# Seven products in place of eight for three of eight K pairs of the first MLP product and, in two passes over the columns, for six of 32 K pairs of the second

## The chip, the cores and the metric

One Trainium2 chip, one of its cores. The metric is the device time of one execution in microseconds (us); lower is better. The core has TensorE (PE, with its weight loads as PEld), VectorE (DVE), ScalarE (ACT), GpSimd (POOL) and SyncE (SP), which here only issues DMAs.

## The reference, cut to what matters

A layer of a streaming encoder on 256 tokens with D = 2048: an RMSNorm, a token mixer (two groups of eight heads each), an output projection, and then the squared-ReLU MLP, which is all that the change touches:

```python
h = h + hybrid_token_mixer(rms_norm(h, norm_mix_w), ...)      # 256 x 2048
n = rms_norm(h, norm_ffn_w)
h = h + jnp.square(jax.nn.relu(n @ w_ff1)) @ w_ff2            # 2048 -> 8192 -> 2048
return rms_norm(h, norm_final_w)
```

Everything is float32. The two MLP products have 256 x 2048 x 8192 multiplications each.

## The kernel before, in words

**A float32 product as three.** TensorE multiplies in the rounded format fp32r. The kernel splits each float32 operand into `hi`, a copy that ACT rounds (line 120), and `lo = w - hi`, which DVE computes (line 121), and adds hi·hi + lo·hi + hi·lo. One *product* below (`product`, lines 774 to 778) is these three matmuls of 128 x 128 weights against 512 columns into one PSUM bank. `split_pair` (its `split` has lines 120 and 121) splits 1024 columns of weights into a pair of buffers; five such pairs are used in turn, three from `spool` and two from `wp2`. So a split may run ahead of TensorE by as much as five pairs hold.

**Order.** A scheduler of the framework orders each engine's instructions when the kernel is built; on the chip each engine runs its own list in that order, and semaphores hold an instruction until its operands and buffers are there. Weights come as 1 MB tiles (`w`, three buffers), one DMA each from SP's queue.

**First MLP product** (lines 805 to 868). Eight column groups `ng` of 1024 columns; in each, eight K pairs `kp` of 256 rows, one weight tile each. A *plain pair* (`plain_quad`) takes eight products: two K halves by two token halves (128 rows) by two column halves (512). A *sum pair* (`kp` in `SUMS = (2, 5)`, lines 834 to 862) treats the same work as a 2 x 2 by 2 x 2 block product and takes seven products of sums of blocks, in the manner of Strassen and Winograd. For its weights DVE computes differences of its blocks, 2048 columns in all (`TT`, lines 840, 843 and 844), and 3584 columns have to be split instead of 2048: three pairs and one half pair `hi4`, `lo4`. The sums of activation blocks are made once (`blocks`, lines 713 to 734; the DVE lines 729 to 732): those of kp 0 to 3 during the output projection, those of kp 4 to 7 in the first group, where `fill` slips them between the products. Four of the seven products go to four PSUM banks `M` of their own, three go directly into the four banks `E` of the plain pairs; after the last sum pair, ACT copies one bank and DVE joins the four (lines 858 to 862), and at the group's end DVE adds each `E` bank (line 865). ReLU and a transpose with a square (`turn`, lines 783 to 790) leave the activations for the second product in `g`. `E` and `M` change their PSUM halves (`acc`, `accb`) from group to group.

**Second MLP product** (lines 870 to 945). 64 K tiles `f` of 128 rows, one weight tile of 2048 columns each, all eight banks as sums: 24 matmuls per tile (`ff2`, line 896), no sum pairs. The activations of a tile are split to `gs` (256 columns, lines 120 and 121). The last three tiles are held back (`held`, `TAIL = 3`), so that the sums are finished bank by bank: for token half 0 four banks, for token half 1 three banks and the last one in two pieces of 256 columns, nine matmuls each.

**The end.** For each finished bank `piece` (lines 947 to 952) adds to `h`, squares and weights; `row_rstd` takes the row's scale (with a power on POOL, line 963), `scaled` multiplies and issues the output DMAs (lines 967 to 972).

Of the kernel before, what the change touches and what calls it, by code (L numbers as in the profile page):

```python
# [7 lines left out]
F32 = mybir.dt.float32  # L8
F32R = mybir.dt.float32r
# [6 lines left out]
P = 128  # L16
# [59 lines left out]
def hybrid_block(ctx: ExitStack, tc: tile.TileContext, x, xt, w_in, w_ab, params, w_out, w_ff1, w_ff2,  # L76
# [594 lines left out]
    wp2 = ctx.enter_context(tc.tile_pool(name="wp2", bufs=2, side="right"))  # L671
    t1 = ExitStack()
# [12 lines left out]
    SUMS = (2, 5)  # L685
    sets = bpool.tile([P, 8192], F32R, tag="xT", name="sets")
    sets2 = tp.tile([P, 1792], F32R, tag="s2", name="sets2")
# [83 lines left out]
    def g(f, n=1):  # L771
        return gt[f // NG][:, f % NG:f % NG + n, :]
# [10 lines left out]
    def turn(ng, n, src, acc):  # L783

        half, hf = n // 2, n % 2
        pt = acc()
        for c in range(4):
            PE.transpose(pt[:, c * P:(c + 1) * P], src[:, c * P:(c + 1) * P], ident)  # L788
        ACT.activation(g(8 * ng + 4 * half, 4)[:, :, hf * P:(hf + 1) * P], pt.rearrange("p (c t) -> p c t", c=4),
                       AF.Square)  # L790

    def plain_quad(E, st, B, first, last, n_fill):

        def one(n, kk):
            hf, c = divmod(n, 2)
            a = [st[:, kk, s + hf * P:s + hf * P + P] for s in (0, T)]
            product(E[n], a, B[kk][c], first and kk == 0, last and kk == 1)

        for n, kk in [(n, kk) for n in range(4) for kk in range(2)] if last else \
                [(n, kk) for kk in range(2) for n in range(4)]:  # L800
            one(n, kk)
            if (n, kk) == (3, 0):
                fill(n_fill)

    c1 = ExitStack()
    for ng in range(NGR):
# [5 lines left out]
        for kp in range(KP):  # L812
            w = wtile()
            SP.dma_start(w, w_ff1[ng * KP + kp])
            if kp not in SUMS:
                B12, B11 = halves(split_pair(w[:, 0:1024]))
                B21, B22 = halves(split_pair(w[:, 1024:2048]))
                plain_quad(E, a_plain(kp), ((B11, B12), (B21, B22)), kp == 0, kp == KP - 1, 0 if kp == 0 else 2)
                if kp == 0:
                    fill(2)  # L820
                if ng == 0 and kp == 1:
# [8 lines left out]
                    gt += [fp.tile([P, NG, T], F32, tag=f"g{i}", name=f"g{i}") for i in range(2)]  # L830
# [5 lines left out]
            TT = tp.tile([P, 2048], F32, tag="TT", name="TT")  # L836
            B = [w[:, c * 512:(c + 1) * 512] for c in range(4)]
            T1, T2, T4 = [TT[:, c * 512:(c + 1) * 512] for c in (0, 2, 3)]
            B21, B22 = halves(split_pair(w[:, 1024:2048]))
            DVE.tensor_tensor(out=TT[:, 0:1024].rearrange("p (a c) -> p a c", a=2), in0=view(w, 0, [[1536, 2], [1, 512]]),  # L840
                              in1=view(w, 512, [[-512, 2], [1, 512]]), op=ALU.subtract)
            B1, B3 = halves(split_pair(TT[:, 0:1024]))
            DVE.tensor_tensor(out=T2, in0=B[3], in1=T1, op=ALU.subtract)
            DVE.tensor_tensor(out=T4, in0=B[2], in1=T2, op=ALU.subtract)
            B2, B4 = halves(split_pair(TT[:, 1024:2048]))
            B11 = [tp.tile([P, 512], F32R, tag=t, name=t) for t in ("hi4", "lo4")]
            split(B[1], None, *B11)
            st = a_sums(kp)
            A = [(st[:, 0, n, :], st[:, 1, n, :]) for n in range(7)]
            p1, p5, p6, p7 = M  # L850
            a0, z0 = kp == SUMS[0], kp == SUMS[-1]
            for dst, a, b in ((E[0], 1, B21), (E[1], 6, B22), (p5, 3, B1), (p7, 5, B3), (p6, 4, B2), (E[2], 2, B4),
                              (p1, 0, B11)):
                m = a in (0, 3, 4, 5)
                product(dst, A[a], b, a0 and m, z0 and m)
            if z0:
                C4 = cp.tile([P, 4, 512], F32, tag="C", name="C4")
                ACT.copy(C4[:, 0], p1)
                DVE.tensor_tensor(out=C4[:, 1], in0=p6, in1=C4[:, 0], op=ALU.add)
                DVE.tensor_tensor(out=C4[:, 2], in0=p5, in1=C4[:, 1], op=ALU.add)  # L860
                DVE.tensor_tensor(out=C4[:, 3], in0=p7, in1=C4[:, 2], op=ALU.add)
                DVE.tensor_tensor(out=C4[:, 1], in0=p7, in1=C4[:, 1], op=ALU.add)
# [13 lines left out]
    accs = [[None] * 4, [None] * 4]  # L876

    def columns(q, bank):
        for hf in range(2):
            for c in (2 * q, 2 * q + 1):  # L880
                accs[hf][c] = bank()

    columns(0, bank_m)
    TAIL = 3
    held = []

    def ff2(f, hf, c, gs, hl, fresh=None):

        hi, lo = hl[c // 2]
        at, n = (c % 2) * 512, 512  # L890
        dst, first, last = accs[hf][c], f == 0, f == (NF - TAIL - 1 if (hf, c) == (1, 3) else NF - 1)
        if fresh:
            dst, at = fresh[0], at + fresh[1]
            n, first, last = 256, f == NF - TAIL, f == NF - 1
        for a, ww in ((0, hi), (T, hi), (0, lo)):
            PE.matmul(dst, lhsT=gs[:, a + hf * P:a + hf * P + P], rhs=ww[:, at:at + n],  # L896
                      start=(first and a == 0 and ww is hi), stop=(last and ww is lo))

    keep = None
    late = []  # L900
    for f in range(NF):
        w = wtile()
        SP.dma_start(w, w_ff2[f])
        gs = f2.tile([P, 2 * T], F32R, tag="gs", name="gs", bufs=4)
        split(g(f)[:, 0, :], None, gs[:, 0:T], gs[:, T:])
        n = f - (NF - TAIL)
        if n == 0:
            keep = fp.tile([P, TAIL - 1, 2, D], F32R, tag="g0", name="keep")
        if f < 2:

            hl = [split_pair(w[:, 0:1024]), None]
            for hf in range(2):
                for c in range(2):
                    ff2(f, hf, c, gs, hl)
                    fill(f == 0 and hf == 1)
            fill(2)
            late.append((f, gs, w))
            if f == 1:
                columns(1, bank_e)
                c1.close()  # L920
                for f_, gs_, w_ in late:
                    hl = [None, split_pair(w_[:, 1024:2048])]
                    for hf in range(2):
                        for c in (2, 3):
                            ff2(f_, hf, c, gs_, hl)
            continue
        hl = []
        for q in range(2):
            qs = slice(q * 1024, (q + 1) * 1024)
            if 0 <= n < TAIL - 1:  # L930
                hl.append(split(w[:, qs], None, keep[:, n, 0, qs], keep[:, n, 1, qs]))
            else:
                hl.append(split_pair(w[:, qs]))
        if n >= 0:
            held.append((f, gs, hl))
            continue
        for q in range(2):
            for hf in range(2):
                for c in (2 * q, 2 * q + 1):
                    ff2(f, hf, c, gs, hl)  # L940
# [111 lines left out]
```

## Time and profile before

| | |
|---|---|
| median of 3 runs | 1253.52 us (1253.51 to 1253.60) |
| profiled execution, its own time | 1253.56 us |
| its span in the trace | 1251.9 us |
| mean granted TensorE clock | 0.995 of full speed |
| matmuls in the program's MLP products, by the loops | 1488 in the first, 1545 in the second (18 of them with 256 columns) |

Matmuls are pipelined: a record of 0.39 us overlaps the next, and what one matmul costs is the distance between starts. The span is 1.66 us shorter than the execution's time; the sums below are made on the execution's own time.

### The profile page before, as it was taken

The numbers are of one execution on the slowest core, as the hardware profiler recorded it, in microseconds if no ns is written. First come the engines' busy times: TensorE is split into PE (matmuls) and PEld (weight loads), VectorE is DVE, ScalarE is ACT, GpSimd is POOL, SyncE is SP. The second block draws the span as 40 slices with busy tenths as digits, with TensorE's granted clock in tenths as the row PEclk, the third lists the DMA queues.
The fourth block names the chain that finished last, engine by engine and source line by source line (L and its number), as shares of the span: only waits on it lengthen the run. The fifth ranks groups of instructions, "written<-read, shape, count | busy, mean of one in ns | idle before, by whom it ended". The sixth has DMA issues, their size and how long they took to land.

```text
span 1251.9 us, 18221 instructions
## 1 busy us (share of the span) xinstructions
PE 1227.6 (98%) x7117; PEld 1030.5 (82%) x7117; DVE 905.1 (72%) x1237; ACT 715.9 (57%) x1016; POOL 134.5 (11%) x184
## 2 busy tenths in 40 slices
PE   7999999998999999999999999999999999999997
PEld 5888888887888887888888888888888888888886
DVE  7788999888789986687767767777655555555565
ACT  7567667765677765565555555555644444444452
POOL 1243433262011120000000000000000000000000
PEclk9999999998999999999999999999999999999999
DMA  8455555543335445656454555545655555555551
GB/s 313 154 163 189 173 180 177 183 165 110 134 126 212 169 169 184 229 193 234 177 194 168 202 192 205 204 174 200 269 203 200 199 184 193 199 199 185 191 198 68
DMA packets 36710, 233.45 MB, mean 186 GB/s; under 512 B 4648, under 2 KB 5680, under 8 KB 9616
## 3 DMA queue, kind: packets, MB, share of 16 engines
q1 hardware_dynamic: 34416, 229.83, 51.6%
q0 software_dynamic: 1632, 1.72, 1.2%
q8 instruction: 56, 0.92, 0.3%
q10 hardware_dynamic: 576, 0.74, 0.2%
q14 instruction: 30, 0.25, 0.1%
HBM read 227.67 MB, written 4.60 MB: 186 GB/s over the span
## 4 chain that ended last, share of the span: by engine, by line
PE 92%; DMA 2%; DVE 2%; POOL 1%; issue 1%; ACT 1%; SPq 0%; POOLq 0%; DVEq 0%; ACTq 0%
PE acc L291 16%; PE acc L896 14%; PE accb L896 14%; PE acc L292 8%; PE accb L776 4%; PE acc L777 4%; PE acc L776 4%; PE acc L778 4%; PE accb L777 4%; PE accb L778 4%; PE accb L750 4%; PE acc L750 3%; DVE lo L121 1%; POOL X L433 1%; PE acc L788 1%
## 5 line engine op out<-in xcount | busy, mean ns | idle before, releaser
L121 DVE TENSOR_TENSOR lo<-w,hi 128x1024 fp32r<-128x1024 f32 (+1 forms) x416 | 504.0, 1217 | 252.2 <-ACT hi L120 244.3
L120 ACT CAST hi<-w 128x1024 fp32r<-128x1024 f32 (+1 forms) x416 | 425.1, 1026 | 350.2 <-PE accb L896 94.9
L291 PE MATMUL acc<-xT,hi 128*128 128x512 f32 x1024 | 361.2, 399 | 6.5 <-ACT hi L120 6.1
L292 PE MATMUL acc<-xT,lo 128*128 128x256 f32 x1024 | 282.6, 284 | 2.1 <-DVE lo L121 2.1
L291 PEld LDWEIGHTS acc<-xT,hi 128*128 128x128 f32 x1024 | 190.4, 189 | 46.6 <-ACT hi L120 6.9
L292 PEld LDWEIGHTS acc<-xT,lo 128*128 128x128 f32 x1024 | 193.9, 190 | 9.1 <-DVE lo L121 4.6
L896 PE MATMUL acc<-hi,gs 128*128 128x512 f32 (+1 forms) x500 | 153.8, 389 | 0.0
L896 PE MATMUL accb<-hi,gs 128*128 128x512 f32 x494 | 151.7, 389 | 0.0
L896 PEld LDWEIGHTS acc<-hi,gs 128*128 128x128 f32 x500 | 93.5, 188 | 19.1
L896 PEld LDWEIGHTS accb<-hi,gs 128*128 128x128 f32 x494 | 92.7, 188 | 19.3
L776 PE MATMUL acc<-hi,sets 128*128 128x512 f32 x248 | 97.2, 392 | 0.0
L776 PE MATMUL accb<-hi,sets 128*128 128x512 f32 x248 | 97.2, 392 | 0.0
L896 PE MATMUL acc<-lo,gs 128*128 128x512 f32 (+1 forms) x250 | 97.1, 388 | 0.0
L778 PE MATMUL accb<-lo,sets 128*128 128x512 f32 x248 | 96.5, 389 | 0.0
L777 PE MATMUL acc<-hi,sets 128*128 128x512 f32 x248 | 96.5, 389 | 0.0
L777 PE MATMUL accb<-hi,sets 128*128 128x512 f32 x248 | 96.5, 389 | 0.0
L778 PE MATMUL acc<-lo,sets 128*128 128x512 f32 x248 | 96.2, 389 | 0.0
L896 PE MATMUL accb<-lo,gs 128*128 128x512 f32 x247 | 95.8, 389 | 0.0
L963 POOL TENSOR_TENSOR fin<-fin,cst 128x1 f32<-128x1 f32 x2 | 1.1, 565 | 760.7 <-DVE fin L962 760.7
L121 DVE TENSOR_TENSOR lo<-TT,hi 128x1024 fp32r<-128x1024 f32 x32 | 39.1, 1225 | 37.1 <-ACT hi L120 35.4
L120 ACT CAST hi<-TT 128x1024 fp32r<-128x1024 f32 x32 | 33.5, 1047 | 38.0 <-issue 13.1
L896 PEld LDWEIGHTS acc<-lo,gs 128*128 128x128 f32 x250 | 46.9, 188 | 9.7
(310 smaller groups left out, 1584.2 us busy)
## 6 DMA issues: line engine op xcount, KB each, us to landing
w<-in_w_ff_dram SPq DMA_DIRECT2D x128, 1024.0 KB, 4.9
w<-in_w_in_dram SPq DMA_DIRECT2D x62, 1024.0 KB, 4.9
w<-in_w_out_dram SPq DMA_DIRECT2D x16, 1024.0 KB, 4.9
big<-in_xt_dram SPq DMA_DIRECT2D x8, 256.0 KB, 5.7
w<-in_w_in_dram SPq DMA_DIRECT2D x8, 256.0 KB, 5.8
h<-in_x_dram SPq DMA_DIRECT2D x2, 1024.0 KB, 5.9
scr_h<-h SPq DMA_DIRECT2D x4, 512.0 KB, 6.2
tail<-scr_h SPq DMA_DIRECT2D x2, 1024.0 KB, 5.9
```

Of the source, the lines that this page charges most:

```text
L120: ACT.copy(hi, w)
L121: eng.tensor_tensor(out=lo, in0=w, in1=hi.bitcast(F32), op=ALU.subtract)
L291: PE.matmul(accs[g], lhsT=hi[:, kk, g, :], rhs=xT[:, k, :], start=(k == 0), stop=False)
L292: PE.matmul(accs[g][:, T:], lhsT=lo[:, kk, g, :], rhs=xT[:, k, 0:T], start=False, stop=(k == KT - 1))
L433: POOL.tensor_tensor(out=X[:, j + 1:, 0:ncol], in0=X[:, j + 1:, 0:ncol], in1=t3, op=ALU.subtract)
L750: PE.matmul(accs[2 * hf + c], lhsT=st, rhs=ww[:, c * 512:(c + 1) * 512], start=(k == 0 and a == 0 and ww is hi), stop=(k == 2 * NH - 1 and ...
L776: PE.matmul(dst, lhsT=ah, rhs=bh, start=start, stop=False)
L777: PE.matmul(dst, lhsT=al, rhs=bh, start=False, stop=False)
L778: PE.matmul(dst, lhsT=ah, rhs=bl, start=False, stop=stop)
L788: PE.transpose(pt[:, c * P:(c + 1) * P], src[:, c * P:(c + 1) * P], ident)
L896: PE.matmul(dst, lhsT=gs[:, a + hf * P:a + hf * P + P], rhs=ww[:, at:at + n], start=(first and a == 0 and ww is hi), stop=(last and ww is lo))
L963: POOL.tensor_tensor(out=r, in0=r, in1=C("nhalf"), op=ALU.pow)
```

## The change

In the first product `SUMS` becomes `(2, 4, 6)`: three sum pairs of eight in each group. The body of a sum pair becomes the function `sum_quad` and the joining of its banks `joins`; the tiles `TT`, `hi4` and `lo4` move to a pool `tq` that lives through both products.

The second product is rewritten to the form of the first: two passes `q` of 1024 columns, each over 32 K pairs of 256 rows, with one weight tile of 1 MB per pair (the weights are laid out anew on the host, 64 tiles as before). Six pairs in each pass (`SUMS2`) are sum pairs; for these DVE makes the sums of activation blocks (128 x 128) in the loop, and the activations are split in every pass. The squares are stored in `g` in another order. The last two pairs of a pass are held back, so that the banks are finished one by one, 12 matmuls each.

```diff
-    SUMS = (2, 5)
+    SUMS = (2, 4, 6)
...
+    def sum_quad(E, M, A, w, a0, z0):
+        TT = tq.tile([P, 2048], F32, tag="TT", name="TT")
+        B = [w[:, c * 512:(c + 1) * 512] for c in range(4)]
+        T1, T2, T4 = [TT[:, c * 512:(c + 1) * 512] for c in (0, 2, 3)]
+        B21, B22 = halves(split_pair(w[:, 1024:2048]))
+        DVE.tensor_tensor(out=TT[:, 0:1024]..., in0=view(w, 0, [[1536, 2], [1, 512]]),
+                          in1=view(w, 512, [[-512, 2], [1, 512]]), op=ALU.subtract)
+        B1, B3 = halves(split_pair(TT[:, 0:1024]))
+        DVE.tensor_tensor(out=T2, in0=B[3], in1=T1, op=ALU.subtract)
+        DVE.tensor_tensor(out=T4, in0=B[2], in1=T2, op=ALU.subtract)
+        B2, B4 = halves(split_pair(TT[:, 1024:2048]))
+        B11 = [tq.tile([P, 512], F32R, tag=t, name=t) for t in ("hi4", "lo4")]
+        split(B[1], None, *B11)
+        p1, p5, p6, p7 = M
+        for dst, a, b in ((E[0], 1, B21), (E[1], 6, B22), (p5, 3, B1), (p7, 5, B3), (p6, 4, B2), (E[2], 2, B4),
+                          (p1, 0, B11)):
+            m = a in (0, 3, 4, 5)
+            product(dst, A[a], b, a0 and m, z0 and m)
+
+    def joins(M):
...
+        ACT.copy(C4[:, 0], p1)
+        DVE.tensor_tensor(out=C4[:, 1], in0=p6, in1=C4[:, 0], op=ALU.add)
+        DVE.tensor_tensor(out=C4[:, 2], in0=p5, in1=C4[:, 1], op=ALU.add)
+        DVE.tensor_tensor(out=C4[:, 3], in0=p7, in1=C4[:, 2], op=ALU.add)
+        DVE.tensor_tensor(out=C4[:, 1], in0=p7, in1=C4[:, 1], op=ALU.add)
+        return C4
...
-    TAIL = 3
-    for f in range(NF):
-        w = wtile()
-        SP.dma_start(w, w_ff2[f])
-        gs = f2.tile([P, 2 * T], F32R, tag="gs", name="gs", bufs=4)
-        split(g(f)[:, 0, :], None, gs[:, 0:T], gs[:, T:])
...
+    SUMS2 = (3, 7, 11, 15, 19, 23)
+    TAIL = 2
+    KP2 = NF // 2
+    def a2_plain(kp):
+        gs = f2.tile([P, 2, 4, P], F32R, tag="gs", name="gs", bufs=3)
+        split(g(kp).rearrange("p (n t) -> p n t", n=4), None, gs[:, 0], gs[:, 1])
+        return lambda kk, hf: (gs[:, 0, AT[kk][hf]], gs[:, 1, AT[kk][hf]])
+    def a2_sums(kp):
+        X, S = g(kp).rearrange("p (n t) -> p n t", n=4), f2.tile([P, 4, P], F32, tag="S", name="S")
+        DVE.tensor_tensor(out=S[:, 0], in0=X[:, 0], in1=X[:, 3], op=ALU.add)
+        DVE.tensor_tensor(out=S[:, 1], in0=S[:, 0], in1=X[:, 1], op=ALU.subtract)
+        DVE.tensor_tensor(out=S[:, 2], in0=X[:, 1], in1=X[:, 0], op=ALU.subtract)
+        DVE.tensor_tensor(out=S[:, 3], in0=X[:, 2], in1=S[:, 1], op=ALU.subtract)
+        st = f2.tile([P, 2, 7, P], F32R, tag="st", name="st")
+        split(X[:, 1:4], None, st[:, 0, 0:3], st[:, 1, 0:3])
+        split(S, None, st[:, 0, 3:7], st[:, 1, 3:7])
+        return [(st[:, 0, n], st[:, 1, n]) for n in range(7)]
+    for q in range(2):
+        bank_e, bank_m = bank_m, bank_e
+        E = [bank_e() for _ in range(4)]
+        for kp in range(KP2):
+            w = wtile()
+            SP.dma_start(w, w_ff2[q * KP2 + kp])
+            if kp in SUMS2:
...
+                sum_quad(E, M, a2_sums(kp), w, kp == SUMS2[0], kp == SUMS2[-1])
+                if kp == SUMS2[-1]:
+                    C4 = joins(M)
+                    for n in range(4):
+                        add_to_h(n % 2, q * 1024 + n // 2 * 512, C4[:, n])
...
+                continue
+            A, B = a2_plain(kp), plain_weights(w)
+            if kp >= KP2 - TAIL:
+                held.append((kp, A, B))
+                continue
+            plain_quad(E, A, B, kp == 0, False, 2 if kp == 1 else 0, q == 1 and kp == KP2 - TAIL - 1)
...
+        if q == 0:
+            for n in range(4):
+                finish(n)
...
+    for c in (2, 3):
+        finish(c - 2)
+        piece(0, c, c * 512, (c + 1) * 512, E[c - 2])
     s = row_rstd(0, 3, 3)()
...
-    for c in range(3):
-        for f, gs, hl in held:
-            ff2(f, 1, c, gs, hl)
-        piece(1, c, c * 512, (c + 1) * 512, accs[1][c])
+    finish(2)
+    piece(1, 2, 1024, 1536, E[2])
     for n in range(2):
         bank = bank_m()[:, 0:256]
-        for f, gs, hl in held:
-            ff2(f, 1, 3, gs, hl, fresh=(bank, n * 256))
+        finish(3, n * 256, 256, bank)
         piece(1, 3 + n, 1536 + n * 256, 1792 + n * 256, bank)
```

## Rows read from the trace of the kernel before

**Rows 1.** The page's first two parts: busy time of the engines, and the span in 40 slices of 31.3 us, where a digit is a busy share in tenths and PEclk the granted TensorE clock.

```profile
PE 1227.6 (98%) x7117; PEld 1030.5 (82%) x7117; DVE 905.1 (72%) x1237; ACT 715.9 (57%) x1016; POOL 134.5 (11%) x184
PE   7999999998999999999999999999999999999997
DVE  7788999888789986687767767777655555555565
PEclk9999999998999999999999999999999999999999
```

**Rows 2.** The chain of work that ended last, its shares of the span by engine.

```profile
PE 92%; DMA 2%; DVE 2%; POOL 1%; issue 1%; ACT 1%; SPq 0%; POOLq 0%; DVEq 0%; ACTq 0%
```

**Rows 3.** Busy time by stretch: from and to (us), length, then busy us and count of PE, PEld, DVE, ACT and POOL, the granted clock, DMA's share and GB/s. The first row lies in the token mixer; 541.30 is the first matmul of the first MLP product, 892.70 the first of the second. The second row is group 0 of the first product, the third and fourth a middle and the last group, then the second product up to its end phase.

```profile
100.00:200.00 100.00, 100.00 (x561) 85.66 (x560) 93.12 (x127) 70.62 (x100) 40.59 (x49) 1.00 0.55 177
...
541.30:584.00 42.70, 42.70 (x198) 35.52 (x197) 35.25 (x48) 25.87 (x34) 0.00 (x0) 1.00 0.64 222
...
671.00:715.00 44.00, 44.00 (x204) 36.62 (x203) 32.69 (x35) 24.44 (x29) 0.00 (x0) 1.00 0.52 192
...
847.00:892.70 45.70, 45.70 (x212) 38.01 (x211) 33.47 (x38) 26.84 (x35) 0.00 (x0) 1.00 0.49 179
892.70:1226.00 333.30, 333.30 (x1480) 276.10 (x1479) 173.42 (x186) 152.34 (x191) 0.00 (x0) 1.00 0.57 200
```

**Rows 4.** The same chain in order of time, in the second product: start (us), length, engine, tile written, line, number of matmuls. The first and the last of 27 pieces of 12 matmuls that follow each other without a gap.

```profile
932.98 2.72 PE acc L896 x12
...
1003.70 2.72 PE acc L896 x12
```

**Rows 5.** Who waited for whom from 541 to 1226 us, on all engines: total us, times, longest.

```profile
DVE lo L121 <- ACT hi L120: 229.8, 167, 3.3
ACT hi L120 <- PE accb L896: 94.9, 56, 3.3
ACT hi L120 <- PE acc L896: 76.8, 59, 1.4
ACT hi L120 <- PE accb L777: 49.9, 52, 1.9
ACT hi L120 <- PE acc L777: 47.4, 50, 1.9
...
ACT hi L120 <- DMA w<-in_w_ff_dram: 12.1, 8, 2.5
DVE TT L840 <- DMA w<-in_w_ff_dram: 2.8, 2, 1.9
```

**Rows 6.** DVE's instructions from 541 us on, by line and shape: out<-in, shapes, count, busy us in total, mean ns of one, idle time before them and what ended it.

```profile
L121 DVE TENSOR_TENSOR lo<-w,hi 128x1024 fp32r<-128x1024 f32 x232 | 282.9, 1224 | 199.5 <-ACT hi L120 194.4
L121 DVE TENSOR_TENSOR gs<-g,gs 128x256 fp32r<-128x256 f32 x64 | 26.4, 418 | 0.5 <-ACT gs L120 0.5
L840 DVE TENSOR_TENSOR TT<-w 128x1024 f32<-128x1024 f32 x15 | 18.3, 1221 | 2.8 <-DMA w<-in_w_ff_dram 2.8
...
L844 DVE TENSOR_TENSOR TT<-w,TT 128x512 f32<-128x512 f32 x15 | 10.3, 687 | 0.2
L121 DVE TENSOR_TENSOR lo<-w,hi 128x512 fp32r<-128x512 f32 x15 | 10.3, 686 | 0.0
...
L171 DVE SCALAR_TENSOR_TENSOR sets<-accb,prm,sets 128x256 fp32r<-128x256 f32 x6 | 2.9, 478 | 0.0
...
L121 DVE TENSOR_TENSOR sets<-X,sets 128x896 fp32r<-128x896 f32 x1 | 1.1, 1084 | 0.0
...
L729 DVE TENSOR_TENSOR X<-X 128x128 f32<-128x128 f32 x1 | 0.3, 284 | 0.0
```

**Rows 7.** ACT's instructions from 541 us on, in the same columns.

```profile
L120 ACT CAST hi<-w 128x1024 fp32r<-128x1024 f32 x232 | 244.3, 1054 | 258.7 <-PE accb L896 94.9 <-PE acc L896 76.8 <-PE accb L777 36.6
...
L120 ACT CAST hi<-w 128x512 fp32r<-128x512 f32 x15 | 9.3, 618 | 11.8 <-DMA w<-in_w_ff_dram 11.3 <-PE accb L777 0.5
...
L858 ACT COPY C<-accb 128x512 f32<-128x512 f32 x4 | 2.3, 574 | 0.0
```

**Rows 8.** DVE's instructions in order of time around the end of group 0: start (us), length, line, operation, out<-in, number; in brackets the idle time before it and what ended it. L859 to L862 are the joins, L865 the adds at the group's end.

```profile
570.70 5.30 DVE L121 TENSOR_TENSOR lo<-w,hi 128x1024 fp32r<-128x1024 f32 x4 [1.50 <-ACT hi L120]
575.92 0.68 DVE L859 TENSOR_TENSOR C<-accb,C 128x512 f32<-128x512 f32 x1
...
582.58 0.68 DVE L865 TENSOR_TENSOR C<-acc,C 128x512 f32<-128x512 f32 x1
```

**Rows 9.** The end of the kernel in order of time, all engines, in the columns of rows 8.

```profile
1240.85 0.88 PE L896 MATMUL acc<-keep,gs 128*128 128x256 f32 x6
1241.05 0.75 DVE L949 SCALAR_TENSOR_TENSOR tail<-accb,fs,tail 128x512 f32<-128x512 f32 x1 [0.15 <-PE accb L896]
...
1241.84 0.69 DVE L951 SCALAR_TENSOR_TENSOR o<-tail 128x512 f32<-128x512 f32 x1
...
1241.92 0.88 PE L896 MATMUL acc<-keep,gs 128*128 128x256 f32 x6
...
1242.88 0.28 PE L896 MATMUL acc<-lo,gs 128*128 128x256 f32 x1
...
1243.20 0.48 DVE L949 SCALAR_TENSOR_TENSOR tail<-acc,fs,tail 128x256 f32<-128x256 f32 x1 [0.28 <-PE acc L896]
```

**Rows 10.** The DMA issues of the MLP weights: count, size, median us from issue to landing; and what SP's queue waited for between 541 and 1226 us before it issued them (line 814 first product, line 903 second).

```profile
w<-in_w_ff_dram SPq DMA_DIRECT2D x128, 1024.0 KB, 4.9
...
SPq L903 <- DVE lo L121: 304.4, 62, 10.5
SPq L814 <- DVE lo L121: 298.5, 58, 14.6
```

More of the change, by code (lines that the diff above doesn't have):

```diff
@@ L788, in turn, with plain_quad @@
             PE.transpose(pt[:, c * P:(c + 1) * P], src[:, c * P:(c + 1) * P], ident)
-        ACT.activation(g(8 * ng + 4 * half, 4)[:, :, hf * P:(hf + 1) * P], pt.rearrange("p (c t) -> p c t", c=4),
-                       AF.Square)
-    def plain_quad(E, st, B, first, last, n_fill):
+        kp = 4 * ng + 2 * half
+        ACT.activation(view(g(kp), (0 if hf else P), [[4 * P, 2], [3 * P if hf else P, 2], [1, P]]),
+                       pt.rearrange("p (a k t) -> p a k t", a=2, k=2), AF.Square)
+    def plain_quad(E, A, B, first, last, n_fill=0, last3=False):
         def one(n, kk):
             hf, c = divmod(n, 2)
-            a = [st[:, kk, s + hf * P:s + hf * P + P] for s in (0, T)]
-            product(E[n], a, B[kk][c], first and kk == 0, last and kk == 1)
+            product(E[n], A(kk, hf), B[kk][c], first and kk == 0, (last or last3 and n == 3) and kk == 1)
         for n, kk in [(n, kk) for n in range(4) for kk in range(2)] if last else \
@@ L829, in hybrid_block @@
                     fp = ctx.enter_context(tc.tile_pool(name="fp", bufs=1))
[L830 removed]
+                    gt += [fp.tile([P, NG // 2, 4 * P], F32, tag=f"g{i}", name=f"g{i}") for i in range(2)]
                     cp = c1.enter_context(tc.tile_pool(name="cp", bufs=1))
@@ L835, in hybrid_block @@
                 M = [bank_m() for _ in range(4)]
[L836 to L847, printed above, removed]
-            st = a_sums(kp)
[L849 to L862, printed above, removed]
+            st = a_sums(kp)
+            sum_quad(E, M, [(st[:, 0, n, :], st[:, 1, n, :]) for n in range(7)], w, kp == SUMS[0], kp == SUMS[-1])
+            if kp == SUMS[-1]:
+                C4 = joins(M)
         for at, p in ((0, E[0]), (2, E[1]), (1, E[2]), (3, E[3])):
@@ L874, in hybrid_block @@
     SP.dma_start(nfw, norm_final_w.unsqueeze(0).to_broadcast([P, D]))
[L876 to L883, printed above, removed]
-    TAIL = 3
[L885 to L897, printed above, removed]
@@ L899, in hybrid_block @@
-    keep = None
-    late = []
-    for f in range(NF):
-        w = wtile()
-        SP.dma_start(w, w_ff2[f])
-        gs = f2.tile([P, 2 * T], F32R, tag="gs", name="gs", bufs=4)
-        split(g(f)[:, 0, :], None, gs[:, 0:T], gs[:, T:])
[L906 to L940, printed above, removed]
@@ L948, in piece @@
+    def piece(hf, n, a, b, acc, with_o=True):
         hv = h[:, hf, a:b]
@@ L972, in scaled @@
         (ACT if eng is ACT else SP).dma_start(out[0, hf * P:(hf + 1) * P, a:b], h[:, hf, a:b])
-    hv = h[:, 1, 1536:2048]
-    DVE.scalar_tensor_tensor(out=hv, in0=accs[1][3], scalar=fs[:, 7:8], in1=hv, op0=ALU.mult, op1=ALU.add)
-    for c in range(4):
-        for f, gs, hl in held:
-            ff2(f, 0, c, gs, hl)
-        piece(0, c, c * 512, (c + 1) * 512, accs[0][c])
+    SUMS2 = (3, 7, 11, 15, 19, 23)
[5 more added lines that the diff above has]
+        return lambda kk, hf: (gs[:, 0, AT[kk][hf]], gs[:, 1, AT[kk][hf]])
```

67 lines of the change are left out of this document (54 added, 13 removed).

## The prediction

> **What bounds the kernel now.** I read the page first: PE is busy for 98% of the span, DVE for 72%, and from slice 18 on, where the MLP lies, PE shows 9 in every slice but the last while DVE falls to 7 and then 5 [rows 1]. The chain that ended last is 92% PE [rows 2]. Busy PE can hide gaps, because the records overlap, so I looked at stretches and at the starts. In every stretch of both MLP products PE is busy for the whole length at a granted clock of 1.00, the 2.4 GHz level, and DVE for 74% of a middle group of the first product (32.69 of 44.00 us), 83% of group 0 and 52% of the second product [rows 3]. In the chain, 26 pieces of 12 matmuls lie between the starts 932.98 and 1003.70: 70.72 / 312 = 0.2267 us from one matmul to the next [rows 4]. Finally the waits: DVE's largest wait is for ACT's `hi`, and ACT waits for PE to release a pair of buffers, 171.7 us in the second product and 97.3 in the first; for the weights' DMA it is 12.1 us, and nothing on PE stands in the list [rows 5]. So the splits run ahead as far as the five pairs of buffers let them, and PE's number of matmuls sets the time. A change is worth 0.2267 us for every matmul it removes, until DVE can no longer stay ahead.
>
> **Matmuls removed.** A plain pair is 8 x 3 = 24 matmuls, a sum pair 21. First product: one more sum pair in each of 8 groups removes 24. Second product: 64 tiles x 24 = 1536 become 2 x (26 x 24 + 6 x 21) = 1500, so 36 less. Together 60 x 0.2267 = **13.60 us**, all on PE, which sets the end. The last piece in halves: 18 matmuls of 256 columns become 24. Nine of them took 1241.92 - 1240.85 = 1.07 us, 0.119 each, against 0.113 for half of a full one [rows 9]; twelve such halves instead of nine cost 6 x 0.006, 0.03 us. Transposes keep their number.
>
> For this term the Trainium skill has another price: "TensorE: Matmul & The Clock Gate", section "Wait — 56ns, not 53.3ns?", gives 215.7 ns from start to start for 512 columns at the high clock, by which the term would be 12.9 us. The trace has 226.7 ns, and the measurement decides.
>
> **DVE work added to the first product.** A plain pair costs DVE 2 x 1.224 = 2.45 us; a sum pair three splits of 1024 (3.67), a half split (0.69) and the subtractions 1.221 + 2 x 0.687 = 2.60, together 6.96 [rows 6]. PE takes 5.44 and 4.76 us. So DVE is 2.20 us short in a sum pair and 2.99 us over in a plain one. Now sum and plain alternate (2, 4, 6), and each sum pair is repaid by the plain pair behind it. Per group DVE rises by 4.51 us to 32.69 + 4.51 = 37.2 us of 44.0 - 0.68 = 43.3: 86%. In the token mixer DVE was busy for 93.12 of 100 us with PE busy throughout [rows 3]; that is the nearest row to such a load, so I take **nothing** lost in groups 1 to 7. ACT gains a copy of 1024 and one of 512, 1.7 us a group, on 24.4 of 44 [rows 3, 7].
>
> **Joins one pair later.** The joins now stand between kp 6 and 7, where two plain pairs followed before. Until the next group needs those banks lie 24 x 0.2267 = 5.44 us. ACT's copy takes 0.574 [rows 7], four joins 4 x 0.687 = 2.75 (by their like in rows 6); even with one split behind them (1.22) that is 4.55 us. In the trace the joins were put behind four splits and started without a wait [rows 8]. Cost 0; if all of it lay ahead of the splits that the next group needs, 0.9 us would be left as cover.
>
> **Group 0** is the tight one. It gets a sum pair (4.51) and a block of sums instead of a plain one: 4 x 0.284 + 1.084 - 2 x 0.478 = 1.26 [rows 6]. 35.25 + 4.51 + 1.26 = 41.0 of 42.7 - 0.68 = 42.0 us [rows 3]: 98%. Part of the 35.25 is run-ahead into group 1 (the splits at the end of rows 8), which can shrink without loss. Bounds: nothing, if the run-ahead gives it all, and 6.4 us, if DVE's 7.45 idle us of that stretch stay as they are (41.0 + 7.45 - 42.0). It is nearer to the first, as the row of 93% with no PE idle shows: I take **1.0 us**.
>
> **The second product.** Weights: the same 64 DMAs of 1 MB in SP's queue, landing in 4.9 us; SP waits for the splits that free a buffer, not the other way round [rows 10]. Per plain pair DVE now has 2.45 + 0.69 for 512 activation columns = 3.13 us; per sum pair 6.96 + 4 x 0.284 + two activation splits (0.69 for 512; 384 columns between 0.42 and 0.69, say 0.55) = 9.34 [rows 6]. PE 5.44 and 4.76. Three plain pairs and a sum pair: 18.7 of 21.1 us, 89%, still below the 93% row; the deficit of 4.6 us is repaid at 2.3 us per plain pair. Joins and their four adds to `h` (5.8 us) come at the sixth sum pair, with nine plain or held pairs behind them in the pass. So **nothing** lost in the steady state; upper bound in the rivals. Splitting the activations twice lies in these sums.
>
> **Between the passes** four of the five pairs of buffers are held. PE has 48 matmuls there (10.9 us) and needs one new pair at the end of them, which the fifth supplies. The second follows when the first held pair is released, 9 matmuls (2.0 us) before the end; ACT's 1.05 and DVE's 1.22 make it ready 0.2 us after the end, and it is needed 2.7 us after. Cost 0.
>
> **The end.** From the last matmul on the chain is the same. Ahead of it PE has, between token half 0's last matmul and its own last, 12 full and 24 half matmuls (5.6 us), before 27 and 18 (8.3 us). DVE has the row scale, three scalings and now one piece of 1.44 (0.75 + 0.69) instead of three [rows 9]. Between 0 and 1 us late; I take **0.4**.
>
> **Sum:** 1253.56 - 13.60 + 0.03 + 1.0 + 0.4 = 1241.4; the median of the runs is 0.04 below the profiled execution: **1241.3 us**.
>
> **Rivals.**
> (1) *Part is given back in group 0.* For it: 98% load and DVE waits there for PE and a late weight DMA (1.9 us, the longest of DVE's in rows 5). Against: PE was never idle there, although its sums were made in the loop too. With the upper bound, 5.4 us more than I take: 1246.7.
> (2) *DVE becomes the bound at the sum pairs; slower.* Place: the splits of each sum pair, if their order or the five pairs of buffers, of which a sum pair takes three, keep DVE from working ahead. Price when fully exposed: first product 24 x 2.20, second 12 x 4.58, together 108 us, against 13.6 gained. It decides from an eighth of that on. With a quarter exposed, 27 - 13.6: 1267. Against: today 16 sum pairs are hidden with no PE wait, and DVE stands still for 229.8 us in the MLP because it is ahead [rows 5]; of the 333.3 - 173.4 = 160 us that it is not busy in the second product [rows 3], the change asks 2 x (26 x 3.13 + 6 x 9.34 + 5.8) - 173.4 = 113.
> (3) *The gain is eaten at the turns; no change.* Queue order: DVE runs its list in order, so joins or adds that wait for PE hold back every split behind them. At ten turns (eight groups, two passes) 1.4 us each would cancel the gain: 1253.6. Against: rows 8, where joins and adds wait for nothing because splits lie ahead of them. The Trainium skill has this rule, "TensorE: Matmul & The Clock Gate", section "Architectural detail: the array is 16× 32×32, not 1× 128×128": ACT and DVE are strict FIFO queues, while PE may pull weight loads ahead. The trace agrees in that DVE's list is run in order; that it costs here, no row shows.
>
> **How the numbers follow.** The forecast 0.70; rival (1) 0.17; rival (3) 0.05; rival (2) 0.08. A measurement of this kernel can tell 0.2%, 2.5 us, from no change. The forecast and rival (1) are faster, together 0.87; no change 0.05; slower 0.08. The range: its low end is the sum with nothing lost, 1239.9, less 0.7 for a shorter end; its high end takes in rival (1) with a little beyond, 1248. Outside lie rivals (2) and (3) and a few in a hundred.
>
> **What would show it.** PE's starts stay 0.2267 us apart and PE busy in every middle stretch; the first product's span falls from 351.4 us to about 347, the second's to its end phase by some 8 us; DVE near 86% there and 85 to 90% in the first 24 pairs of each pass; joins without idle time ahead of them. Wrong would be: PE waiting for `lo` or `hi` of a sum pair (rival 2), a gap behind kp 7 or at the pass's turn (rival 3), or a gap in group 0 alone (rival 1). A fall of the granted clock inside the MLP would mean that PE was starved.

## The result: 1240.9 us, 1.1% faster

The changed kernel takes 1240.89 us (median of 5 runs, 1238.95 to 1241.58), the kernel before 1253.6 in the same comparison; the ratio is 0.9892, with a 95% interval from 0.9879 to 0.9905. The forecast was 1241.3. The profiled execution took 1239.9 us, its span is 1238.2; it is the second shortest of the five, so below stages are compared in the traces, and totals by medians. (The first matmul of the second product before starts at 892.91 us; at the 892.70 of rows 3 its weights are loaded.)

The page of the changed kernel, its first two parts:

```profile
PE 1215.0 (98%) x7060; PEld 1019.3 (82%) x7060; DVE 1026.5 (83%) x1415; ACT 767.9 (62%) x1071; POOL 134.2 (11%) x184
PE   7999999998999999999999999999999999999997
DVE  7789999878789996778898898889888786887875
PEclk9999999998999999999999999999999999999999
```

PE is as full as before [rows 1], only shorter. DVE, at 5 to 7 tenths in the MLP before, is now at 8 and 9. Busy time by stretch of the changed kernel, in the columns of rows 3: the first product from group 1 to its end, then the first 128 us and a later 140 us of the second:

```profile
583.00:887.00 304.00, 304.00 (x1397) 252.15 (x1396) 259.20 (x280) 185.99 (x221) 0.00 (x0) 1.00 0.56 194
887.00:1015.00 128.00, 128.00 (x574) 106.06 (x573) 106.93 (x140) 77.90 (x98) 0.00 (x0) 1.00 0.60 215
...
1060.00:1200.00 140.00, 140.00 (x619) 115.99 (x618) 117.58 (x143) 83.20 (x103) 0.00 (x0) 1.00 0.59 204
```

PE is busy from end to end at the high clock, while DVE has gone from 74% to 85% of the first product (259.20 of 304) and from 52% to 84% in these two stretches of the second (106.93 of 128 and 117.58 of 140). The waits from 541 to 1226 us, against rows 5:

```profile
DVE lo L121 <- ACT hi L120: 92.7, 100, 1.7
ACT hi L120 <- PE acc L781: 79.6, 88, 1.9
ACT hi L120 <- PE accb L781: 74.6, 85, 2.3
...
ACT hi L120 <- DMA w<-in_w_ff_dram: 23.6, 15, 3.2
...
DVE TT L820 <- DMA w<-in_w_ff_dram: 7.3, 14, 1.9
```

DVE's wait for ACT fell from 229.8 to 92.7 us: that is the idle time the new work went into. ACT still waits for PE to release buffers, so the splits are still ahead, and no wait of PE is in the list. The waits for weights have doubled; they come back below.

Stage by stage, from starts of matmuls in the two profiled executions:

| stage | before, us | after, us | difference | by the count of matmuls |
|---|---|---|---|---|
| up to the first product | 541.30 | 541.09 | -0.21 | 0 |
| first product | 351.61 | 346.75 | -4.86 | -5.44 |
| second product, to its last matmul's start | 349.98 | 341.93 | -8.05 | -8.13 |
| from there to the end | 8.97 | 8.39 | -0.58 | 0 |

### The profile page after: what moved, and what is told of

Same layout as the page of the kernel before. It is cut to its first block, busy times and chain, and to the rows that moved or that the text cites. A ratio compares the mean times of both kernels' runs of the same rounds, so it can differ in the third digit from the quotient of the medians.

```text
span 1238.2 us, 18421 instructions
## 1 busy us (share of the span) xinstructions
PE 1215.0 (98%) x7060; PEld 1019.3 (82%) x7060; DVE 1026.5 (83%) x1415; ACT 767.9 (62%) x1071; POOL 134.2 (11%) x184
## 4 chain that ended last, share of the span: by engine, by line
PE 92%; DVE 2%; DMA 2%; POOL 2%; issue 1%; ACT 1%; SPq 0%; POOLq 0%; DVEq 0%; ACTq 0%
PE acc L291 16%; PE acc L781 9%; PE acc L782 9%; PE acc L780 9%; PE accb L781 9%; PE accb L780 9%; PE accb L782 9%; PE acc L292 8%; PE accb L751 4%; PE acc L751 4%; DVE lo L121 1%; PE accb L792 1%; PE acc L792 1%; POOL Xt L431 1%; PE pk L374 1%
## 5 line engine op out<-in xcount | busy, mean ns | idle before, releaser
L121 DVE TENSOR_TENSOR lo<-w,hi 128x1024 fp32r<-128x1024 f32 (+1 forms) x420 | 498.2, 1193 | 129.9 <-ACT hi L120 120.6
L120 ACT CAST hi<-w 128x1024 fp32r<-128x1024 f32 (+1 forms) x420 | 420.4, 1006 | 276.9 <-PE acc L781 64.9
L121 DVE TENSOR_TENSOR lo<-TT,hi 128x1024 fp32r<-128x1024 f32 x72 | 87.4, 1224 | 26.5 <-ACT hi L120 23.3
L120 ACT CAST hi<-TT 128x1024 fp32r<-128x1024 f32 x72 | 75.1, 1052 | 42.1 <-PE acc L781 14.7
L781 PE MATMUL accb<-hi,sets 128*128 128x512 f32 x244 | 95.4, 391 | 0.0
L780 PE MATMUL accb<-hi,sets 128*128 128x512 f32 x244 | 94.7, 391 | 0.0
L781 PE MATMUL acc<-hi,gs 128*128 128x512 f32 (+1 forms) x216 | 83.3, 386 | 0.0
L780 PE MATMUL acc<-hi,gs 128*128 128x512 f32 (+1 forms) x216 | 83.0, 386 | 0.0
L782 PE MATMUL acc<-lo,gs 128*128 128x512 f32 (+1 forms) x216 | 81.9, 385 | 0.0
L781 PE MATMUL accb<-hi,gs 128*128 128x512 f32 x204 | 79.4, 389 | 0.0
L780 PE MATMUL accb<-hi,gs 128*128 128x512 f32 x204 | 78.7, 389 | 0.0
L782 PE MATMUL accb<-lo,gs 128*128 128x512 f32 x204 | 78.7, 389 | 0.0
L782 PEld LDWEIGHTS acc<-lo,sets 128*128 128x128 f32 x244 | 45.8, 188 | 9.4
```

The lines of the kernel that those rows point to most:

```text
L120: ACT.copy(hi, w)
L121: eng.tensor_tensor(out=lo, in0=w, in1=hi.bitcast(F32), op=ALU.subtract)
L780: PE.matmul(dst, lhsT=ah, rhs=bh, start=start, stop=False)
L781: PE.matmul(dst, lhsT=al, rhs=bh, start=False, stop=False)
L782: PE.matmul(dst, lhsT=ah, rhs=bl, start=False, stop=stop)
```

## The experiments

**One half of the change at a time.** Three kernels:

```diff
# ff1_only: the kernel before with
-    SUMS = (2, 5)
+    SUMS = (2, 4, 6)
# ff2_only: the changed kernel with
-    SUMS = (2, 4, 6)
+    SUMS = (2, 5)
# ff2_form: the changed kernel with
-    SUMS2 = (3, 7, 11, 15, 19, 23)
+    SUMS2 = ()
...
```

`ff1_only` and `ff2_form` also need small edits that do no other work: room for a third set of block sums, and the place where the output tile of half 1 is allotted and weighted.

> First product alone changed (three sum pairs of eight), the second product as before. Theory M (only the number of matmuls counts, PE never waits): 24 fewer, 5.4 us less than before by the count, 4.9 us by the traces' stage: 1248.2 to 1248.8. Rival D (sum pairs cost part of DVE's deficit, and the two-pass form of the second product hides it in the sum): above 1250, with gaps between PE's starts in the groups.

> Second product alone changed (two passes, twelve sum pairs), the first with its two sum pairs as before. Theory M: 36 fewer matmuls, 8.1 us, and up to 0.6 us at the end: 1245.0 to 1246.5. Rival D: 1247 or more. Together with the first product alone the two gains should add up to the whole, 12.7 to 13.7.

> The change without sum pairs in the second product: its two passes over 32 pairs, all plain, so 1536 matmuls there; three sum pairs in the first. Theory M: the changed kernel plus 36 x 0.2267 = 8.2 us, 1249.1, the same as the first product alone within 1 us; DVE's busy time in the second product falls. Rival F (the two-pass form itself gains or costs: activations split twice, two turns, another end): 1247 or less, or 1251 or more.

| kernel | median, us | ratio to before (95%) | first product | second product | after its last matmul |
|---|---|---|---|---|---|
| first product alone | 1249.17 | 0.9964 (0.9951 to 0.9976) | 346.75 | 349.99 | 8.96 |
| second product alone | 1246.39 | 0.9942 (0.9929 to 0.9956) | 351.61 | 341.85 | 8.84 |
| two passes without sum pairs there | 1248.68 | 0.9963 (0.9950 to 0.9975) | 346.75 | 350.06 | 8.38 |

The medians lie within the bands of their totals but for the first, 0.4 us above its band. One more expectation was missed: the two gains, each against the runs of the kernel before beside it, add up to 4.3 + 7.1 = 11.4 us by medians, where 12.7 to 13.7 was expected; the intervals of the two ratios, each about 0.13% (1.6 us) to either side, are too wide to hold this against the sum. The stages say more: each product has its new length whether or not the other is changed, and the two-pass form by itself is worth nothing (350.06 against 349.98): its split of the activations twice, its turn between the passes and its other order cost PE no time. The two products shorten by 4.86 and 8.13 us on their own, 12.99 together. What shortens each product is its sum pairs alone. Nothing of rival F or D shows.

**More sum pairs in the second product.** How much DVE can take is the other half of the reason. `dense9` has nine sum pairs a pass, `dense9b` nine in other places, `dense98` nine and eight:

```diff
-    SUMS2 = (3, 7, 11, 15, 19, 23)
+    SUMS2 = (3, 6, 9, 12, 15, 18, 21, 24, 27)             # dense9
+    SUMS2 = (2, 4, 7, 10, 13, 16, 19, 22, 25)             # dense9b
+    SUMS2 = tuple(range(3, (27, 24)[q] + 1, 3))           # dense98
```

> Nine sum pairs instead of six in each pass of the second product, every third (3, 6, ... 27): 18 matmuls fewer. Theory M with DVE still able to keep up: 4.1 us less than the changed kernel, 1236.8. DVE's occupancy in a cycle of three pairs by the distance between its starts: 13.95 of 15.64 us, 89%. Rival D (DVE's deficit at a sum pair, 4.6 us by busy time, needs more than two plain pairs to be repaid): PE waits and the gain is eaten, 1240 or more.

> Nine sum pairs in each pass at 2, 4, 7, 10, ... 25 instead of 3, 6, ... 27: the same matmuls as with nine at every third, the last sum pair two pairs further from the end. Theory C: the end phase goes back from 9.7 us to 8.4 to 9.0 behind the last matmul, since DVE's joins no longer stand there; the second product stays at 338 to 339 us: 1237.5 to 1238.0. Rival E (the end's length has nothing to do with the last sum pair): 1238.7 as with every third.

> The second product with nine sum pairs in the first pass (3, 6, ... 27) and eight in the second (3, 6, ... 24): 15 matmuls fewer than the changed kernel, 3.4 us, with the first sum pair where the changed kernel has it and the last one well before the end. Theory C: second product 338.5 to 339.5 us, behind its last matmul 8.4 to 9.0 us, 1237.0 to 1238.0 in all. Rival E (at 88 to 90% DVE loses by chance some other microseconds wherever the sum pairs stand): 1239 or more.

| kernel | median, us | ratio to before (95%) | second product | by count | after its last matmul |
|---|---|---|---|---|---|
| dense9 | 1238.72 | 0.9880 (0.9866 to 0.9893) | 338.78 | 337.85 | 9.70 |
| dense9b | 1240.16 | 0.9888 (0.9873 to 0.9903) | 340.93 | 337.85 | 8.43 |
| dense98 | 1237.18 | 0.9868 (0.9853 to 0.9883) | 340.59 | 338.53 | 8.40 |

`dense98` is the best kernel of the study and beats both, by medians 16.6 us against before and 3.7 against the change; it and the change were not timed side by side. None reaches its count. In `dense9` the gain of 4.1 us became 2.2 by the medians: PE waited once, in one step of 1.0 us, and the end is 1.3 us longer. I had put the end down to DVE and the joins of the last sum pair (expectation of `dense9b`); the trace doesn't bear that out. DVE stood idle for 4.57 us before it took up the first of the last banks, waiting for PE, and did so 4.4 us before the last matmul; in the changed kernel it does so 6.6 us before:

```profile
1222.42 1.41 DVE L904 SCALAR_TENSOR_TENSOR tail<-accb,fs,tail 128x512 f32<-128x512 f32 x2 [4.57 <-PE accb L782]
```

```profile
1223.14 0.75 DVE L904 SCALAR_TENSOR_TENSOR tail<-accb,fs,tail 128x512 f32<-128x512 f32 x1 [3.33 <-PE accb L782]
```

(The last matmuls start at 1226.79 and 1229.77 us.) The scheduler had mixed the last matmuls of these banks, so that they were finished later and the scalings of half 0 stand behind the last matmul. Moving the last sum pair forward did give the end back (8.43 and 8.40), as expected, and the 6.6 us with it; but with sum pairs at 2 and 4 `dense9b` has one step of 2.8 us on PE at 911 us, where PE waits for a `hi`, and its total missed the expectation by 2 us. (That `hi` stands in ACT's list behind an activation split that waited 3.09 us for PE.) In `dense98`, whose second product was expected at 338.5 to 339.5, PE has two long steps, 1.3 and 0.9 us. The first of them on PE, and what DVE did before it:

```profile
1003.63 0.39 PE L781 MATMUL acc<-hi,gs 128*128 128x512 f32 x1
1004.96 0.50 PE L782 MATMUL acc<-lo,gs 128*128 128x512 f32 x1 [0.94 <-DVE lo L121]
```

```profile
999.04 0.69 DVE L121 TENSOR_TENSOR gs<-g,gs 128x512 fp32r<-128x512 f32 x1
1002.54 1.23 DVE L820 TENSOR_TENSOR TT<-w 128x1024 f32<-128x1024 f32 x1 [2.82 <-DMA w<-in_w_ff_dram]
1003.69 1.22 DVE L121 TENSOR_TENSOR lo<-w,hi 128x1024 fp32r<-128x1024 f32 x1
```

DVE was not short of time at this moment: it stood idle for 2.82 us. At the head of its list was the next sum pair's subtraction, whose weights had not landed; behind it stood the split that PE needed. This is the queue order that rival (3) feared, with a DMA at its head in place of a join, and in this stretch DVE is 89% busy (113.56 of 128 us). The one step of `dense9` has the same form, with 2.27 us of waiting for weights. The load itself was late, and DVE has its part in that: SP issued it at 994.88 us, as one of DVE's splits released the buffer, and it landed at 1002.45; DVE had worked from 985.41 to 999.73 us all but without a pause (14.24 of 14.32 us). Whether a fourth weight buffer or another order of the list would give the time back was not tested.

**More DVE work, the same matmuls.**

```diff
+        for _ in range(3):
             DVE.tensor_tensor(out=TT[:, 0:1024]..., op=ALU.subtract)
```

> The changed kernel with the first subtraction of every sum pair (1024 columns, 1.14 us by starts) made three times instead of once, the same result: 2.3 us more of DVE at each of 36 sum pairs, nothing else. Theory C: in the second product DVE goes from 81% to about 91%, PE hides it but for a gap or two, 342 to 344 us; in the first product 36.6 + 6.8 = 43.4 of 43.3 us a group, full, so PE begins to wait: 347 to 360 us. Together 1241 to 1256. Rival 2 of the prediction (DVE's work at a sum pair lies on the path): 36 x 2.3 = 82 us more, 1323.

Measured: 1256.22 us, 1.0019 of before (1.0010 to 1.0028), 0.2 above the band of theory C. The first product grew by 13.0 us to 359.75, the second by 1.2 to 343.12, as theory C had it and far from rival 2's 82 us. Busy time of the first product, of two stretches of the second:

```profile
583.00:890.00 307.00, 300.10 (x1362) 244.23 (x1361) 290.70 (x307) 170.43 (x210) 0.00 (x0) 1.00 0.52 186
900.00:1030.00 130.00, 129.52 (x578) 106.46 (x577) 123.03 (x158) 78.21 (x99) 0.00 (x0) 1.00 0.61 224
1060.00:1220.00 160.00, 160.00 (x708) 132.53 (x707) 141.52 (x168) 91.11 (x116) 0.00 (x0) 1.00 0.57 200
```

With DVE at 88% (last row) PE loses nothing, at 95% in the second product about a microsecond, and at 95% in the first product, where groups end every 43 us, some 1.6 us a group. So 82 us of added DVE work cost 14 in the two products, and the changed kernel, at 84 to 85%, stands a few per cent of DVE's time below the point where PE begins to pay, with the work in this order; another order pays earlier, as shown below.

**Fewer buffers to run ahead with.**

```diff
-        pool, t = (spool, "") if n % 5 < 3 else (wp2, "2")
+        pool, t = (spool, "")
-    TAIL = 2
+    TAIL = 1
```

> Three pairs of buffers for the split weights instead of five, and one pair of K rows held back at a pass's end instead of two. A sum pair takes all three. Theory C: a pair is released half a plain pair before the sum pair's third product needs its own, so little is lost: the steady stretches of the second product within 3 us of 341.9 less what the end shifts, 1241 to 1246. Rival B (the run-ahead of five pairs is what hides the sum pairs): 1 to 3 us at each of 36 sum pairs, 1275 to 1350.

Measured: 1246.52 us, 0.9942 (0.9925 to 0.9958), above the band of theory C by half a microsecond; but the products take 346.59 and 341.87 us, and PE waits nowhere in them:

```profile
583.00:887.00 304.00, 304.00 (x1398) 252.78 (x1398) 253.52 (x278) 187.33 (x221) 0.00 (x0) 1.00 0.55 196
887.00:1060.00 173.00, 173.00 (x772) 143.29 (x771) 141.02 (x182) 101.03 (x124) 0.00 (x0) 1.00 0.60 215
```

Three pairs of buffers hide the sum pairs as well as five. The loss is all behind the last matmul, which starts at 1230.27 us: 14.13 instead of 8.39 us. DVE takes up the first of the last banks only 1.3 us before that matmul, three of them at once, having waited for PE; the changed kernel does so 6.6 us before:

```profile
1228.94 2.07 DVE L904 SCALAR_TENSOR_TENSOR tail<-accb,fs,tail 128x512 f32<-128x512 f32 x3 [3.14 <-PE accb L782]
```

So the banks are no longer finished one by one: the last matmuls of three of them start within half a microsecond, and almost all of DVE's work on them, the scalings of half 0 too, comes behind the last matmul. Two things were changed at once; whether the held pair or the number of buffers put the matmuls in this order was not tested.

**The place of the sum pairs in the first product.**

```diff
-    SUMS = (2, 4, 6)
+    SUMS = (4, 5, 6)
```

> First product with its three sum pairs in a row (4, 5, 6) instead of alternating (2, 4, 6); the same matmuls, the same DVE work in a group. Theory C (DVE runs ahead over a whole group; only its share, 85%, counts): as the changed kernel, 1240.9 within 1.5, the first product 346.7 us. Rival A (a sum pair has to be repaid by the plain pair directly behind it): three in a row leave DVE 3 x 1.6 (by starts) to 3 x 2.2 us (by busy time) behind, 5 to 7 us a group in eight groups, less the run-ahead of one or two pairs: 1255 to 1280, with gaps of PE behind kp 5 and 6.

Measured: 1251.91 us, 0.9982 (0.9973 to 0.9991): 11 us of the gain are gone, by the same matmuls and the same DVE work. Theory C is refuted; that is nearer to rival A, though below its band. The first product takes 354.56 us, with five steps of 1.3 to 2.0 us on PE at the ends of groups, and 3.3 more at the head of the second. ACT and PE at the end of group 0:

```profile
583.02 2.00 ACT L120 CAST hi<-w 128x1024 fp32r<-128x1024 f32 x2 [3.95 <-DMA w<-in_w_ff_dram]
584.92 0.58 ACT L838 COPY C<-accb 128x512 f32<-128x512 f32 x1
```

```profile
583.84 0.39 PE L782 MATMUL acc<-lo,sets 128*128 128x512 f32 x1
585.55 0.50 PE L780 MATMUL accb<-hi,sets 128*128 128x512 f32 x1 [1.33 <-ACT C L838]
```

PE waits for the bank that ACT's copy at the joins sets free, and that copy stands in ACT's list behind two splits whose weights came late, 3.95 us of waiting. ACT's waits for weights in the first product are 38.2 us against 10.3 in the changed kernel. The trace puts the late weights down to DVE. SP issued the load at 577.90 us, as one of DVE's splits released the buffer, and it landed at 582.92. Up to then DVE had no time left: from 559.21 to 580.74 us it was busy for 21.42 of 21.53.

```profile
559.21 1.22 DVE L121 TENSOR_TENSOR lo<-TT,hi 128x1024 fp32r<-128x1024 f32 x1
...
576.65 4.09 DVE L121 TENSOR_TENSOR lo<-w,hi 128x1024 fp32r<-128x1024 f32 x4
584.11 2.36 DVE L121 TENSOR_TENSOR lo<-w,hi 128x1024 fp32r<-128x1024 f32 x2 [3.36 <-ACT hi L120]
```

So the debt of DVE that rival A named is there, but it shows at the end of the group and not behind kp 5 and 6: a weight buffer is released late, and the joins are the place where that lateness turns into PE time. DVE's share hides it; from group 1 on it is only 83% (251.78 of 304 us), since after the debt it stands idle. So the place of the work in the group counts, not the mean alone. Whether another weight buffer would be enough was not tested.

**Four sum pairs a group, and POOL.**

```diff
-    SUMS = (2, 4, 6)
+    SUMS = (2, 3, 5, 6)                         # first4, first4_pool, all_pool
...
-        split(B[1], None, *B11)
+        split(B[1], None, *B11, eng=POOL)       # first4_pool, all_pool
```

`all_pool` also has the sum pairs of `dense98`.

> Four sum pairs of eight (2, 3, 5, 6) in each group of the first product, the second as in the changed kernel: 24 matmuls fewer, 5.4 us. DVE by starts 40.7 of 42.6 us a group, 95%: between nine sum pairs a pass (88 to 90%, one gap of 0.8 us) and the tripled subtraction (100%, 13 us lost in the first product). Theory C: part of it is given back at the group ends, 1 to 6 us, 1237 to 1241.5. Rival M (only the matmuls count): 1235.5.

> The same, and in every sum pair the half split's lo (512 columns, 0.69 us on DVE) is computed on POOL, which is idle in the MLP. DVE falls to 90% of a first-product group. Theory C (DVE's share sets what is given back): 1235 to 1237.5, and less PE waiting than without POOL. Rival P (POOL, at 2.2 us for 512 columns in the token mixer, is late for the seventh product of a sum pair, or slows DVE): PE waits there, 1242 or more.

> Both together: four sum pairs a group in the first product, nine and eight in the passes of the second, the half split's lo on POOL. Theory C: 24 and 15 matmuls fewer than the changed kernel, 8.8 us, less what DVE at 90% gives back: 1232 to 1235. Rival P: 1239 or more.

| kernel | median, us | ratio to before (95%) | first product | second product |
|---|---|---|---|---|
| first4 | 1244.80 | 0.9924 (0.9912 to 0.9936) | 349.35 | 343.49 |
| first4_pool | 1251.44 | 0.9983 (0.9974 to 0.9992) | 355.16 | 344.08 |
| all_pool | 1260.39 | 1.0050 (1.0031 to 1.0068) | 359.05 | 352.10 |

Four sum pairs remove 5.4 us of matmuls and give back 9.3: slower than the change, and beyond my band of 1 to 6. DVE is 91% busy in the first product (279.52 of 307 us from group 1 on). Groups 2 to 6 have two steps of 0.5 us each on PE. In the second of group 2, PE waits for a `hi` that ACT makes as soon as DVE's subtraction is done, and DVE had run up to there from 657.67 us without a pause:

```profile
667.43 0.68 DVE L824 TENSOR_TENSOR TT<-w,TT 128x512 f32<-128x512 f32 x1
668.15 1.05 ACT L120 CAST hi<-TT 128x1024 fp32r<-128x1024 f32 x1 [0.21 <-DVE TT L824]
669.26 0.50 PE L780 MATMUL accb<-hi,sets 128*128 128x512 f32 x1
```

So here it is DVE's work itself that is late. The remedy was worse still: theory C is refuted for POOL, and rival P holds, by its second clause (DVE slowed down; no wait of PE for POOL is in the list). DVE's 512-column subtractions in `first4_pool`, and without POOL in `first4`:

```profile
L823 DVE TENSOR_TENSOR TT<-w,TT 128x512 f32<-128x512 f32 x43 | 41.2, 959 | 0.7
```

```profile
L823 DVE TENSOR_TENSOR TT<-w,TT 128x512 f32<-128x512 f32 x43 | 29.5, 686 | 0.2
```

The same 43 instructions take 40% longer on average, and one of them beside POOL's:

```profile
611.91 1.80 POOL L121 TENSOR_TENSOR lo<-w,hi 128x512 fp32r<-128x512 f32 x1 [3.42 <-ACT hi L120]
612.60 1.66 DVE L824 TENSOR_TENSOR TT<-w,TT 128x512 f32<-128x512 f32 x1
```

The subtraction that usually takes 0.69 us starts inside POOL's 1.80 us and ends 0.55 us after it. In the first product POOL takes 31 half splits of 0.686 us off DVE, 21 us; DVE's other splits and subtractions of the sum and plain pairs become some 25 us longer in exchange. The Trainium skill names such a conflict: "GPSIMD Engine Reference", section "1. Specifications", has the SBUF interfaces of GpSimd shared with VectorE, with contention for DVE instructions that have two SBUF inputs. The rows above agree: the subtraction has two SBUF inputs and takes 1.66 us for 0.69.

## Why the prediction was right, step by step

- **The bound.** Right, and it carries everything: a product's length follows its matmuls. In the changed kernel the turn between the passes shows the distance, and that nothing waits there:

```profile
1053.17 0.39 PE L781 MATMUL acc<-hi,gs 128*128 128x512 f32 x1
...
1059.74 0.39 PE L780 MATMUL accb<-hi,gs 128*128 128x512 f32 x1
...
1061.78 0.39 PE L780 MATMUL accb<-hi,gs 128*128 128x512 f32 x1
```

  From 1053.17 to 1061.78 lie 38 steps, 0.2266 us each, across the change of banks at 1059.74.
- **Matmuls removed, 13.60 us.** The stages gave 12.91. The second product is right within 0.1; the first is 0.58 short, because seven groups take 43.35 us where 43.95 - 0.68 = 43.27 was due. The transposes of a group now stand in three places instead of two, and each return from them to 512 columns costs some 0.09 us (0.32 from start to start once, for 0.23). That 12.9 equals the sum by the Trainium skill's 215.7 ns ("TensorE: Matmul & The Clock Gate", "Wait — 56ns, not 53.3ns?") is chance: the distance between starts is 226.6 ns here, and the missing part lies at the transposes.
- **DVE's share.** 86% forecast for the first product, 85% measured. In the second 84% measured for 85 to 90: durations overlap when DVE runs without a break (in the rows of the joins below, one of 1.23 us starts at 581.31 and the next at 582.45), so sums of durations come out high. That nothing is lost at such a share was taken from the token mixer's row of 93%. The conclusion came true, but the ground was weak: `first4` loses time at 91% and the three sum pairs in a row at 83%, so a share from another stage can't be carried over. New shapes were priced well: the 512-column activation split took 0.685 us (0.69), 384 columns 0.551 (0.55), a block sum 0.285 (0.284).
- **Group 0, 1.0 us.** Wrong size: it takes 43.30 us against 43.98, 0.68 less, which is the count exactly. I had added 5.8 us to the 35.25 us that DVE is busy in this stretch. In the first 42.02 us, the length that I had allowed, DVE is busy for 37.03:

```profile
541.09:583.11 42.02, 42.02 (x195) 34.96 (x194) 37.03 (x51) 27.76 (x36) 0.00 (x0) 1.00 0.63 223
```

  That is 1.8 more, and 5 us of idle time are left. The rest of the 5.8 is run-ahead that shrank, as the lower bound had it, and what the durations overlap; the two were not told apart.
- **Joins and turns at no cost.** Right. But the joins no longer stand behind all the splits as in rows 8; they are mixed with them:

```profile
580.48 0.68 DVE L839 TENSOR_TENSOR C<-accb,C 128x512 f32<-128x512 f32 x1
581.31 1.23 DVE L820 TENSOR_TENSOR TT<-w 128x1024 f32<-128x1024 f32 x1
582.45 0.68 DVE L840 TENSOR_TENSOR C<-accb,C 128x512 f32<-128x512 f32 x1
...
585.45 0.68 DVE L842 TENSOR_TENSOR C<-accb,C 128x512 f32<-128x512 f32 x1
```

  They end at 586.1 us, in time, but PE writes the fourth of these banks again from 586.43 us on: 0.3 us to spare, less than the 0.9 that I had claimed. The runs with the sum pairs in a row show what happens when they slip. In the second product eight pairs (24 to 31) stand behind the sixth sum pair of a pass, not nine as I had counted; that cost nothing.
- **The end, +0.4 us.** DVE was not late, and the stage came out 0.58 us shorter. Two of half 1's four banks are now finished at the turn of the passes, so DVE has less behind it; that is worth 0.15 us at most, since DVE's last scaling starts 2.38 us behind the last matmul's start and 2.53 before. The rest lies behind that scaling, where only the output is still sent, and this part moves from one run to the next: the second product alone has the same code, the same 2.38 and 8.84 us in all.
- **The sum.** 1241.4 was made for the profiled execution, which took 1239.9: I charged 1.4 us of losses that did not come, the end and the stage ahead of the MLP gave another 0.8, and I missed 0.6 at the transposes. That the median comes within 0.4 us of the forecast is in part luck, since the profiled execution is 1.0 us below the median.
- **The rivals.** None of (1) to (3) shows in the changed kernel. (2) was argued with a run-ahead of five pairs of buffers; three are enough, and 82 us of extra DVE work cost 14. (3) is real as a mechanism, a few microseconds from here: a wait for a DMA or for PE at the head of an in-order list is what PE paid for in the middle of `dense9`, `dense98` and `dense9b`, and a late copy in the kernel with three sum pairs in a row. (2) is near as well: in `first4`, in that kernel and in `dense98` DVE had worked without a pause before it was late.

## What to carry to other kernels

When the engine that sets the end runs without a gap, price a change by instructions times the distance between their starts, and check that the helping engines can take the new work where it lands. Their share alone doesn't tell: here DVE at 88% of a stretch cost nothing, and at 83% with three sum pairs in a row the change lost 11 us. Look for stretches in which the helping engine has no idle time left, and for what it releases late then: a buffer, a load, a bank. In-order lists add to it: a waiting instruction at the head (here weights in flight, or the copy that frees a bank) holds back what the main engine needs next. So spread the extra work evenly, place it where its inputs are early and the banks it frees are not needed at once, and time a second engine beside the first before you move work to it: here POOL slowed DVE by more than it took off it.

## What the runs showed of the hardware that was not expected

- POOL's 512-column subtraction took 1.91 us on average beside DVE, and the 43 subtractions of DVE shown above rose from 0.686 to 0.959 us on average.
- In the kernel with three sum pairs in a row PE stood still for 1.66, 0.75 and 0.30 us at the head of the second product; then, from 898.11 us on, the matmuls came 0.43 us apart for some three microseconds; from 898.10 to 901.00 the granted clock is 0.50, the 1.2 GHz level. Here is the clock of the whole stretch (0.73 granted) and three of the starts:

```profile
895.00:901.00 6.00, 4.63 (x11) 3.27 (x12) 6.00 (x10) 4.34 (x8) 0.00 (x0) 0.73 0.99 414
```

```profile
898.53 0.63 PE L782 MATMUL acc<-lo,gs 128*128 128x512 f32 x1
898.96 0.63 PE L780 MATMUL acc<-hi,gs 128*128 128x512 f32 x1
899.39 0.63 PE L781 MATMUL acc<-hi,gs 128*128 128x512 f32 x1
```

- The stage ahead of the MLP, which no kernel here changes, ended between 539.84 and 542.30 us. That is as much as the smaller differences of this study, and the reason to compare stages. Where it comes from was not looked into.
